# Two PSUM banks trade places in the blocks of 512 columns, and a bank's last two additions become one

## The chip, the cores and the metric

The kernel runs on one core of a Trainium2 chip. A core has a matrix engine (TensorE, PE in the profile, with its weight loads shown apart as PEld), a vector engine (VectorE, DVE), a scalar engine (ScalarE, ACT), a general engine (GpSimd, POOL) and queues that issue DMAs (SyncE, SP). Each engine runs its own list of instructions in order, and waits on semaphores for the others. TensorE writes its sums into PSUM, which holds 128 partitions of eight banks of 512 float32 values; everything else lies in SBUF. The metric is the device time of one execution in microseconds (us): the median of several runs.

## What is computed

One decoder layer on 256 tokens of width 2048, all in float32:

```
hn = rms_norm(x, norm_mix_g);  z = hn @ w_in              # 2048 x 10248
q_a, k_a, v_a, q_b, k_b, v_b, f_logit, g_a, g_b = split(z)
a   = moba_attention(q_a, k_a, v_a) @ w_proj_a            # 8 heads of 128
bfx = forgetting_attention(q_b, k_b, v_b, f_logit) @ w_proj_b
x = x + (sigmoid(g_a) * a + sigmoid(g_b) * bfx) @ w_out
hm = rms_norm(x, norm_mlp_g)
x = x + square(relu(hm @ w_up)) @ w_down                  # 2048 -> 8192 -> 2048
return rms_norm(x, norm_final_g)
```

## The kernel before

**Float32 in three products.** Every matrix product is made of pairs of rounded numbers. A value is split into a high part (a rounding copy, ScalarE, L133 for weights) and a low part (the rest, a VectorE subtraction, L148). `triple` (L324 is its matmul) then issues three matmuls of 128 rows, 128 columns and 512 moving columns: high by high, high by low, low by high. The split weights lie in rings of 12 high slots (`his`) and 10 low slots (`los`) of 512 columns each, so the splitting runs at most ten slots ahead of TensorE. Raw weights come in chunks of 1 MB through three buffers.

**Groups.** The wide products (w_in, w_up) are worked off in groups of 1024 columns. A group is a 2x2 scheme of Strassen's kind: rows are the two halves of the tokens, columns the two halves of 512. It goes through eight pairs of row blocks of the weight. A pair of kind W takes seven triples, one for each of seven PSUM banks P1 to P7, in the order P1, P2, P3, P7, P6, P4, P5 (`SEVEN_P`); of its weights the tiles T1 to T4 are sums that VectorE makes first (L160, L161, L162, `emit_sums`). A pair of kind S takes eight plain triples into P5, P3, P2 and P4. The pairs 0, 2, 4, 6 of the w_up groups are W (pairs 0, 3, 6 for w_in), the last pair is S with its triples in the order P2, P4, P2, P4, P3, P3, P5, P5 (`LAST`). Where a bank gets its last triple, `run_group` emits at once the operations that put the seven banks together to the four quarters of the row tile `c` (token half, column half): L371 on ScalarE, L372 to L381 on VectorE. P5 goes into two quarters, by L380 and L381.

**Blocks.** The narrow products (w_proj_a, w_proj_b, w_out, w_down) are worked off in blocks of 512 output columns: two banks, one for each half of the tokens, and for each 128 rows of weights a triple into the first bank and a triple into the second. The table `BANKS` says which two banks the n-th block takes. When a block is done, VectorE adds its banks to a row tile, first bank first: `proj_evac` (L707, and for the second projection L709 behind each), `out_evac` (L727), `down_part` (L759), and in the last round `final_part` (L763, L765). The eighth bank, `aux`, serves transposes and attention.

**Order.** The order on each engine is written out. `plan` is the list of groups and blocks: six w_in groups for q, k, v of both mixers; then two times two gate groups and four projection blocks (a, a, b, b); four w_out blocks; then four rounds of two w_up groups and one `run_down` of four blocks. `pump` is called after each triple and emits the splitting as soon as slots are free by the order of the program; VectorE then reaches these instructions in the order in which they were emitted. At the end of every pair (after the third and the last triple of a W pair, after the fourth and the last of an S pair) `boundary` emits small tasks that are due, one transpose task among them: after the w_out blocks these are `x1_transpose` (L736), which transposes 256 columns of the row tile that L727 has written.

**Where a block is followed by a group.** This happens five times: the gate groups follow the fourth projection block once, the first w_up group follows the fourth w_out block, and the w_up groups of rounds 2, 3 and 4 follow the fourth w_down block. The group starts with P1, P2, P3, while VectorE still has to add up the two banks of the fourth block. In all five places the fourth block has the banks `BANKS[3]`.

Of the kernel before, what the change touches and what calls it, by code (L numbers as in the profile page):

```python
# [10 lines left out]
OP = mybir.AluOpType  # L11
# [4 lines left out]
NT = 2  # L16
# [39 lines left out]
         ((0, 384, "s"), (768, 640, "v"), (384, 384, "s"), (1408, 640, "v")))  # L56
FF = 16

BANKS = (("P1", "P7"), ("P6", "P2"), ("P4", "P1"), ("P5", "P3"))


@with_exitstack
def hybrid_layer(ctx: ExitStack, tc, x, xt, gcols, w_in, w_f, b_forget, w_proj_a, w_proj_b, w_out,
                 w_up, w_down, norm_final_g, out):
    nc = tc.nc
# [98 lines left out]
    def pump(*freed):  # L164

        used.update(freed)
        while live and live[0] in used:
            used.remove(live.pop(0))
            taken[2] += 1
        go = True  # L170
        while go:
            go = False
            if acts:
                q, i = acts[0]
                names, where, _ = PIECES[chunks[q][0]][i]
                if taken[0] + len(names) - taken[2] <= HI_SLOTS and q in (sums if where else raw):
                    emit_high(q, i)
                    acts.pop(0)
                    go = True
            if dves:  # L180
                q, i = dves[0]
                names, where, _ = PIECES[chunks[q][0]][i]
                n = len(names)
                if taken[1] + n - taken[2] <= LO_SLOTS and taken[1] + n <= taken[0]:
                    emit_low(q, i)
                    dves.pop(0)
                    go = True
                else:

                    c = q + (i == len(PIECES[chunks[q][0]]) - 1)  # L190
                    if not sums and c in raw and c not in added and chunks[c][0] == "W":
                        emit_sums(c)
                        added.add(c)
                        go = True
# [10 lines left out]
    def add_block(what, src, n, k0, nk, banks):  # L205
        q = len(chunks)
        for k in range(k0, k0 + nk, 4):
            add_chunk("N", src, k, n * 512)
        plan.append(("block", what, q, nk // 4, banks))

    def add_proj(c):
        for i, (what, src) in enumerate((("pa", w_proj_a), ("pb", w_proj_b))):
            for n in (2 * c, 2 * c + 1):
                add_block((what, n), src, n, 0, NH, BANKS[2 * i + n % 2])

# [6 lines left out]
    for n in range(4):  # L222
        add_block(("o", n), w_out, n, 0, KT, BANKS[n])
    for f0 in range(0, DFF // 128, FF):
# [80 lines left out]
    def boundary():  # L305
        now[0] += 1
        due = [t for t in tasks if t[0] <= now[0]]
        tasks[:] = [t for t in tasks if t[0] > now[0]]
        for _, f, a in due:
            f(*a)  # L310
        ready = [t for t in queue if t[0] <= now[0]]
        if ready:
            t = min(ready, key=lambda t: t[0])
            queue.remove(t)
            t[1](*t[2])
# [4 lines left out]
    def triple(p, a, w, first, last):  # L320
        (xh, xl), (wh, wl) = a, w
        n = p.shape[-1]
        for j, (l, r) in enumerate(((xh, wh), (xh, wl), (xl, wh))):
            nc.tensor.matmul(p, l, r[:, :n], start=first and j == 0, stop=last and j == 2)  # L324

    def bank(n):
        return psum.tile([128, 512], FT, name=n)
# [11 lines left out]
    def run_group(q, fa, lay, plain, beside=None):  # L339

        flat = []
        for j in range(KP):
            kind = chunks[q + j][0]
            table = {"P": FOUR, "S": LAST if j == KP - 1 else EIGHT, "W": SEVEN_P}[kind]
            half = 2 if kind == "W" else 3
            flat += [(j, w, i, p, m in (half, len(table) - 1)) for m, (w, i, p) in enumerate(table)]
        last = {s[3]: m for m, s in enumerate(flat)}
        last_use = {s[:2]: m for m, s in enumerate(flat)}
        b, done, c = {}, set(), None

        def ready(*names):
            if done.issuperset(names):
                done.difference_update(names)
                return True

        for m, (j, w, i, n, end) in enumerate(flat):
            first = n not in b
            if first:
                b[n] = bank(n)
            triple(b[n], (fa[:, 0, lay.off[j] + i], fa[:, 1, lay.off[j] + i]), split[q + j, w], first, m == last[n])  # L360
            if m == last[n]:
                done.add(n)
            if last_use[j, w] == m:
                used.add((q + j, w))
            if plain:
                if end:
                    beside(j)
            else:
                if ready("P1", "P6", "P7"):
                    c = rows.tile([128, NT, 2, 512], FT, name="row")  # L370
                    nc.scalar.activation(c[:, 0, 1], b["P1"], AF.Copy)  # L371
                    nc.vector.tensor_tensor(c[:, 0, 0], b["P6"], c[:, 0, 1], OP.add)  # L372
                    nc.vector.tensor_tensor(c[:, 1, 0], c[:, 0, 0], b["P7"], OP.subtract)
                if ready("P2", "P4"):
                    nc.vector.tensor_tensor(c[:, 0, 1], c[:, 0, 1], b["P2"], OP.add)
                    nc.vector.tensor_tensor(c[:, 1, 1], c[:, 1, 0], b["P4"], OP.add)
                if ready("P3"):
                    nc.vector.tensor_tensor(c[:, 0, 0], b["P3"], c[:, 0, 0], OP.subtract)
                if ready("P5"):
                    nc.vector.tensor_tensor(c[:, 1, 0], b["P5"], c[:, 1, 0], OP.subtract)  # L380
                    nc.vector.tensor_tensor(c[:, 0, 0], c[:, 0, 0], b["P5"], OP.add)  # L381
            if m < len(flat) - 1:
                if end:
                    boundary()
                pump()
        if plain:
            c = rows.tile([128, NT, 2, 512], FT, name="row")
            for tok, h, n in ((0, 1, "P2"), (1, 1, "P4"), (1, 0, "P5"), (0, 0, "P3")):
                nc.scalar.activation(c[:, tok, h], b[n], AF.Copy)
        return c.rearrange("p t h c -> p t (h c)")  # L390
# [20 lines left out]
    def run_halves(q, act, outs, h0, h1, k0, nk, free=True):  # L411

        for h in range(h0, h1):
            for kk in range(2):
                k = k0 + 2 * (h - h0) + kk
                hi, lo = split[q + h // 2, 2 * (h % 2) + kk]
                for tok, c0, n, p in outs:
                    triple(p[:, :n], (act(k, 0, tok), act(k, 1, tok)),
                           (hi[:, c0:c0 + n], lo[:, c0:c0 + n]), k == 0, k == nk - 1)
                if free:  # L420
                    used.add((q + h // 2, 2 * (h % 2) + kk))
                if kk == 0:
                    pump()
            if h < h1 - 1:
                boundary()
                pump()
# [6 lines left out]
    def whole(ps):  # L433
        return [(tok, 0, 512, ps[tok]) for tok in range(NT)]
# [357 lines left out]
    def run_down(f0, q):  # L792
        act = pair_act(hT, f0 // 2)
        last = f0 + FF == DFF // 128
        ps = [[bank(n) for n in BANKS[i]] for i in range(2)]

        for i, (k, n) in enumerate(((0, 0), (0, 1), (8, 0), (8, 1))):
# [4 lines left out]
            pump()  # L802
        ps = [bank(n) for n in BANKS[2]]
        run_halves(q + 8, act, whole(ps), 0, 8, 0, FF)
        down_evac(2, ps, last)
        boundary()
        pump()
        ps = [bank(n) for n in BANKS[3]]
        if not last:
# [42 lines left out]
    for step, what, q, *more in plan:  # L852
        if step == "group":
            kind, n = what[:2]
            plain = more[0]
            if kind == "up" and n == 0:
                assert not [t for t in queue if t[1] is not x1_transpose]
            c = run_group(q, *((ref["x1T"], FX1) if kind == "up" else (xT, FX)), plain, forget_matmuls if plain else None)
            t0 = now[0] + 1
            if kind == "q":  # L860
# [110 lines left out]
```

## Time and profile before

| What | Value |
|---|---|
| Device time, median of 3 runs | 1377.78 us (1376.17 to 1379.2) |
| Device time of the profiled execution | 1376.19 us |
| Its span, first to last instruction | 1374.2 us |
| TensorE (PE) busy | 1349.2 us, 98% of the span, 6159 matmuls |
| VectorE busy | 1049.0 us, 76%, 1352 instructions |
| ScalarE busy | 790.9 us, 58% |
| DMA | 262.25 MB, mean 191 GB/s |
| Mean granted clock of TensorE | 0.995 of full speed |

The span is 2.0 us shorter than the time of that execution. Busy time of TensorE covers nearly the whole span, so what can go is the idle time of TensorE (25 us) and stretches in which it runs at less than full clock. A wait is charged by the profile to the instruction that released it.

### The profile page before, as it was taken

The page shows a single profiled execution, that of the slowest core. Times are in us where ns is not written, and L with a number is a line of the kernel's source. Part 1 is how long each engine was busy: PE and PEld are TensorE (multiplying, and loading weights), DVE is VectorE, ACT ScalarE, POOL GpSimd, SP SyncE. Part 2 cuts the span into 40 slices and gives each one's busy share as a digit, 9 for nine tenths or more (in the row PEclk, how much of TensorE's full clock was granted, in tenths as well). Part 3 has the DMA queues.
Part 4 walks back from the last instruction along what each step waited for, and adds up shares of the span by engine and source line. Part 5 has one row for each costly group of instructions (what it writes and reads, how often), then busy time and mean ns, then how long its engine had stood idle before and what let it go on. Part 6 is the DMA issues. An engine that isn't in the chain of part 4 may idle for free.

```text
span 1374.2 us, 16641 instructions
## 1 busy us (share of the span) xinstructions
PE 1349.2 (98%) x6159; PEld 1114.4 (81%) x6159; DVE 1049.0 (76%) x1352; ACT 790.9 (58%) x1041; POOL 13.7 (1%) x29
## 2 busy tenths in 40 slices
PE   9999999999999999999999999999999999999997
PEld 7778888888788888888788887888878888788886
DVE  5788988888967886666898567995579955799674
ACT  6766666766664465555676544665446653457532
POOL 0000000000000000000000000000000000000000
PEclk9999999999999999999999999999999999999999
DMA  8556554544565656564557554566545665555651
GB/s 309 183 188 212 184 170 166 184 153 158 184 211 168 209 206 215 201 228 153 170 198 240 184 189 158 187 216 206 186 151 184 217 212 186 180 185 202 232 199 72
DMA packets 93824, 262.25 MB, mean 191 GB/s; under 512 B 4656, under 2 KB 5040, under 8 KB 93104
## 3 DMA queue, kind: packets, MB, share of 16 engines
q1 hardware_dynamic: 92752, 257.97, 55.2%
q10 hardware_dynamic: 992, 3.24, 0.6%
q8 instruction: 48, 0.79, 0.2%
q14 instruction: 32, 0.26, 0.1%
HBM read 259.09 MB, written 2.10 MB: 190 GB/s over the span
## 4 chain that ended last, share of the span: by engine, by line
PE 91%; DVE 3%; ACT 3%; issue 1%; DMA 1%; POOL 0%; SPq 0%; POOLq 0%; ACTq 0%; DVEq 0%
PE P L324 87%; PE aux L667 2%; DMA raw<-in_w_in_dram 1%; ACT his L133 1%; DVE los L148 1%; DVE sum L160 1%; PE aux L641 1%; PE aux L593 0%; PE aux L627 0%; DVE row L759 0%; DVE sum L161 0%; ACT pr L448 0%; ACT row L469 0%; PE aux L642 0%; PE aux L736 0%
## 5 line engine op out<-in xcount | busy, mean ns | idle before, releaser
L324 PE MATMUL P<-his,big 128*128 128x512 f32 x2186 | 706.6, 397 | 12.1 <-DVE row L759 7.0
L133 ACT ACTIVATE his<-raw 128x1024 fp32r<-128x1024 f32 (+1 forms) x525 | 480.6, 932 | 380.0 <-PE P L324 357.8
L148 DVE TENSOR_TENSOR los<-raw,his 128x1024 fp32r<-128x1024 f32 (+1 forms) x579 | 550.0, 983 | 150.1 <-PE P L324 109.4
L324 PEld LDWEIGHTS P<-his,big 128*128 128x128 f32 x2186 | 412.8, 189 | 101.0 <-DVE row L759 8.3
L324 PE MATMUL P<-his,pr 128*128 128x512 f32 (+1 forms) x1568 | 483.5, 387 | 0.0
L324 PE MATMUL P<-los,big 128*128 128x512 f32 x1093 | 427.9, 392 | 0.3 <-DVE los L485 0.3
L324 PEld LDWEIGHTS P<-his,pr 128*128 128x128 f32 x1568 | 292.3, 188 | 58.2
L324 PE MATMUL P<-los,pr 128*128 128x512 f32 (+1 forms) x784 | 302.0, 385 | 0.0
L324 PEld LDWEIGHTS P<-los,big 128*128 128x128 f32 x1093 | 206.7, 189 | 41.4 <-DVE los L485 0.6
L324 PEld LDWEIGHTS P<-los,pr 128*128 128x128 f32 x784 | 147.4, 188 | 28.5
L148 DVE TENSOR_TENSOR los<-sum,his 128x1024 fp32r<-128x1024 f32 (+1 forms) x139 | 143.9, 1060 | 30.2 <-PE P L324 29.0
L133 ACT ACTIVATE his<-sum 128x1024 fp32r<-128x1024 f32 (+1 forms) x129 | 124.8, 981 | 48.2 <-PE P L324 27.9
L160 DVE TENSOR_TENSOR sum<-raw 128x1024 f32<-128x1024 f32 x59 | 72.0, 1221 | 0.4 <-DMA raw<-in_w_up_dram 0.3
L755 DVE TENSOR_TENSOR pr<-tmp,pr 128x512 fp32r<-128x512 f32 x32 | 22.1, 689 | 29.7 <-ACT pr L754 29.7
L161 DVE TENSOR_TENSOR sum<-sum,raw 128x512 f32<-128x512 f32 x59 | 41.7, 706 | 2.0
L162 DVE TENSOR_TENSOR sum<-sum,raw 128x512 f32<-128x512 f32 x59 | 40.8, 692 | 2.0
L667 PEld LDWEIGHTS aux<-ident,row 128*128 128x128 f32 x224 | 28.0, 141 | 9.1 <-ACT cum L566 2.1
L667 PE MATMUL aux<-ident,row 128*128 128x128 f32 x224 | 33.6, 272 | 1.6 <-ACT cum L566 1.6
L752 ACT ACTIVATE tmp<-aux 128x512 f32<-128x512 f32 x32 | 19.2, 599 | 26.3 <-PE aux L667 26.1
L396 DVE TENSOR_TENSOR big<-pr,big 128x512 fp32r<-128x512 f32 (+1 forms) x16 | 10.5, 658 | 23.9 <-ACT big L395 23.9
L759 DVE SCALAR_TENSOR_TENSOR row<-P,inv,row 128x512 f32<-128x512 f32 x24 | 17.1, 749 | 11.0 <-PE P L324 11.0
L407 ACT ACTIVATE big<-pr 128x256 fp32r<-128x256 f32 (+1 forms) x16 | 8.2, 510 | 23.7 <-DVE pr L406 13.9
(133 smaller groups left out, 511.4 us busy)
## 6 DMA issues: line engine op xcount, KB each, us to landing
raw<-in_w_in_dram SPq DMA_DIRECT2D x79, 1024.0 KB, 5.2
raw<-in_w_up_dram SPq DMA_DIRECT2D x64, 1024.0 KB, 5.1
raw<-in_w_down_dram SPq DMA_DIRECT2D x64, 1024.0 KB, 5.2
raw<-in_w_out_dram SPq DMA_DIRECT2D x16, 1024.0 KB, 5.2
raw<-in_w_proj_a_dram SPq DMA_DIRECT2D x8, 1024.0 KB, 5.2
raw<-in_w_proj_b_dram SPq DMA_DIRECT2D x8, 1024.0 KB, 5.2
row<-in_xt_dram SPq DMA_DIRECT2D x8, 256.0 KB, 8.5
row<-in_x_dram SPq DMA_DIRECT2D x2, 1024.0 KB, 7.9
```

The lines of the kernel that those rows point to most:

```text
L133: nc.scalar.activation(his[:, s:s + m], src[:, j:j + m], AF.Copy)
L148: nc.vector.tensor_tensor(los[:, s + jj:s + jj + mm], src[:, j + jj:j + jj + mm], his[:, h:h + mm].bitcast(FT), OP.subtract)
L160: nc.vector.tensor_tensor(t[:, 0:2], r[:, 1:3], r[:, 0:1].to_broadcast([128, 2, 512]), OP.add)
L161: nc.vector.tensor_tensor(t[:, 2], t[:, 0], r[:, 2], OP.add)
L162: nc.vector.tensor_tensor(t[:, 3], t[:, 2], r[:, 3], OP.add)
L324: nc.tensor.matmul(p, l, r[:, :n], start=first and j == 0, stop=last and j == 2)
L396: nc.vector.tensor_tensor(fa[:, 1, o + i:o + 4], f[:, i:4], fa[:, 0, o + i:o + 4].bitcast(FT), OP.subtract)
L641: nc.tensor.matmul(p[:, i * S:(i + 1) * S], v[:, 0, sl], pt[:, :S], start=True, stop=False)
L667: nc.tensor.transpose(p[:, c, s * 128:(s + 1) * 128], src[:, tok, (i + c) * 128:(i + c + 1) * 128], ident)
L752: nc.scalar.activation(t, p, AF.Square)
L755: nc.vector.tensor_tensor(h[:, :, 1], t, h[:, :, 0].bitcast(FT), OP.subtract)
L759: nc.vector.scalar_tensor_tensor(t, p, inv2[:, tok:tok + 1], t, op0=OP.mult, op1=OP.add)
```

## The change

The table `BANKS` gives the third block P3 and P1 instead of P4 and P1, and the fourth block P4 and P5 instead of P5 and P3. In `run_group` the sign of the quarter `c[:, 1, 0]` is turned round, so that the last bank P5 is added to both quarters with the same sign; L380 and L381 become one VectorE operation of 2 x 512 elements, in which P5 is the second operand, repeated along the new axis.

```diff
-BANKS = (("P1", "P7"), ("P6", "P2"), ("P4", "P1"), ("P5", "P3"))
+BANKS = (("P1", "P7"), ("P6", "P2"), ("P3", "P1"), ("P4", "P5"))
...
-                    nc.vector.tensor_tensor(c[:, 1, 0], c[:, 0, 0], b["P7"], OP.subtract)
+                    nc.vector.tensor_tensor(c[:, 1, 0], b["P7"], c[:, 0, 0], OP.subtract)
...
-                    nc.vector.tensor_tensor(c[:, 1, 1], c[:, 1, 0], b["P4"], OP.add)
+                    nc.vector.tensor_tensor(c[:, 1, 1], b["P4"], c[:, 1, 0], OP.subtract)
...
                 if ready("P5"):
-                    nc.vector.tensor_tensor(c[:, 1, 0], b["P5"], c[:, 1, 0], OP.subtract)
-                    nc.vector.tensor_tensor(c[:, 0, 0], c[:, 0, 0], b["P5"], OP.add)
+                    p5 = b["P5"].rearrange("p (o c) -> p o c", o=1).to_broadcast([128, NT, 512])
+                    nc.vector.tensor_tensor(c[:, :, 0], c[:, :, 0], p5, OP.add)
```

**TensorE, from the last w_down block of a round to the w_up group behind it.** `P5_5964` is bank P5 as the block uses it, `P1_6096` bank P1 as the group uses it; in brackets stands the engine whose semaphore the instruction waits for. Of each triple that only goes on, the rows are left out. Before:

```order
L324 MATMUL P5_5964<-his_78,pr_5672 128x512
L324 MATMUL P3_5965<-his_78,pr_5672 128x512
...
L324 MATMUL P1_6096<-his_78,big_4411 128x512 [waits Activation_49]
...
L324 MATMUL P2_6103<-his_78,big_4411 128x512 [waits Activation_49]
...
L324 MATMUL P3_6107<-his_78,big_4411 128x512 [waits DVE_49]
...
L324 MATMUL P7_6113<-his_78,big_4411 128x512 [waits Activation_49]
...
L324 MATMUL P6_6122<-his_78,big_4411 128x512
...
L324 MATMUL P4_6126<-his_78,big_4411 128x512 [waits Activation_49]
...
L324 MATMUL P5_6130<-his_78,big_4411 128x512
```

In the changed kernel the same stretch of TensorE's list reads:

```order
L324 MATMUL P4_5953<-his_78,pr_5661 128x512
L324 MATMUL P5_5954<-his_78,pr_5661 128x512
...
L324 MATMUL P1_6085<-his_78,big_4402 128x512 [waits Activation_49]
...
L324 MATMUL P2_6092<-his_78,big_4402 128x512 [waits Activation_49]
...
L324 MATMUL P3_6096<-his_78,big_4402 128x512
L324 MATMUL P3_6096<-los_79,big_4402 128x512
...
L324 MATMUL P7_6102<-his_78,big_4402 128x512 [waits Activation_49]
L324 MATMUL P7_6102<-los_79,big_4402 128x512 [waits DVE_49]
...
L324 MATMUL P6_6111<-his_78,big_4402 128x512
...
L324 MATMUL P4_6115<-his_78,big_4402 128x512 [waits DVE_49,Activation_49]
...
L324 MATMUL P5_6119<-his_78,big_4402 128x512 [waits DVE_49]
```

The matmuls stand in the same order; the wait for VectorE that stood at the third triple (P3) now stands at the sixth and seventh (P4, P5), and the fourth has a wait of its own for its low part.

**TensorE, from the last w_out block to the first w_up group.** Here a transpose (`aux`, L736) of the row that the block's evacuation writes comes behind the third triple. Before:

```order
L324 MATMUL P3_4918<-his_78,big_4411 128x512 [waits DVE_49]
L324 MATMUL P3_4918<-los_79,big_4411 128x512
L324 MATMUL P3_4918<-his_78,big_4411 128x512
L736 MATMUL aux_4925<-ident_119,row_4322 128x128 [waits PE_49,Activation_49]
L736 MATMUL aux_4925<-ident_119,row_4320 128x128
```

And in the changed kernel:

```order
L324 MATMUL P3_4909<-his_78,big_4402 128x512
L324 MATMUL P3_4909<-los_79,big_4402 128x512
L324 MATMUL P3_4909<-his_78,big_4402 128x512
L736 MATMUL aux_4916<-ident_119,row_4313 128x128 [waits DVE_49,Activation_49]
L736 MATMUL aux_4916<-ident_119,row_4311 128x128
```

The wait for VectorE has moved by one triple, from P3 to the transpose.

**VectorE, at the end of a group.** The piece of the difference at the first group with seven banks; the numbers behind P name the banks' buffers, `P_638` is P5:

```order
-L376 TENSOR_TENSOR row<-row,P_634 128x512
+L376 TENSOR_TENSOR row<-P_634,row 128x512
 L378 TENSOR_TENSOR row<-P_610,row 128x512
 L148 TENSOR_TENSOR los<-sum,his 128x1024
-L380 TENSOR_TENSOR row<-P_638,row 128x512
-L381 TENSOR_TENSOR row<-row,P_638 128x512
```

One instruction of 2 x 512 (L381) stands where two of 512 stood, in each of the 17 groups with seven banks. On VectorE nothing else changes its place, and on ScalarE and SyncE nothing at all.

## Rows read from the trace of the kernel before

**Rows 1.** The page, part 1, and one group of part 5.

```profile
PE 1349.2 (98%) x6159; PEld 1114.4 (81%) x6159; DVE 1049.0 (76%) x1352; ACT 790.9 (58%) x1041; POOL 13.7 (1%) x29
...
L759 DVE SCALAR_TENSOR_TENSOR row<-P,inv,row 128x512 f32<-128x512 f32 x24 | 17.1, 749 | 11.0 <-PE P L324 11.0
```

**Rows 2.** Waits of TensorE: engine line waited for: total us, times, longest.

```profile
PE P L324 <- DVE row L759: 7.0, 3, 2.3
PE P L324 <- DVE row L727: 2.2, 1, 2.2
...
PE P L324 <- DVE row L707: 0.4, 1, 0.4
```

**Rows 3.** Timeline, start of round 2: start, us, engine, line, shapes, [idle before].

```profile
835.37 0.39 PE L324 MATMUL P<-los,pr 128*128 128x512 f32 x1
...
836.05 0.39 PE L324 MATMUL P<-los,pr 128*128 128x512 f32 x1
836.31 1.22 DVE L160 TENSOR_TENSOR sum<-raw 128x1024 f32<-128x1024 f32 x1
...
837.63 0.39 PE L324 MATMUL P<-his,big 128*128 128x512 f32 x1
838.90 1.40 DVE L759 SCALAR_TENSOR_TENSOR row<-P,inv,row 128x512 f32<-128x512 f32 x2
840.22 1.82 DVE L148 TENSOR_TENSOR los<-raw,his 128x1024 fp32r<-128x1024 f32 x2
840.36 0.50 PE L324 MATMUL P<-his,big 128*128 128x512 f32 x1 [2.34 <-DVE row L759]
```

**Rows 4.** Windows: length, busy (x instructions) of each engine, PEclk, DMA share, GB/s.

```profile
840.36:845.03 4.67, 4.67 (x13) 3.67 (x14) 3.50 (x4) 2.10 (x3) 0.00 (x0) 0.63 0.54 174
1017.04:1022.41 5.37, 5.37 (x16) 4.25 (x17) 3.09 (x4) 2.00 (x2) 0.00 (x0) 0.68 0.59 197
1193.73:1198.19 4.46, 4.46 (x19) 3.68 (x20) 4.04 (x5) 2.67 (x3) 0.00 (x0) 1.00 0.46 150
```

**Rows 5.** Timeline, last w_out block and first w_up group.

```profile
661.77 0.39 PE L324 MATMUL P<-his,big 128*128 128x512 f32 x1
663.03 1.28 DVE L727 TENSOR_TENSOR row<-row,P 128x512 f32<-128x512 f32 x2
664.37 0.50 PE L324 MATMUL P<-his,big 128*128 128x512 f32 x1 [2.21 <-DVE row L727]
...
665.17 0.60 PE L736 MATMUL aux<-ident,row 128*128 128x128 f32 x4
```

**Rows 6.** Timeline, last projection block and the gate group behind it.

```profile
440.95 0.39 PE L324 MATMUL P<-his,big 128*128 128x512 f32 x1
440.95 0.68 DVE L707 TENSOR_TENSOR row<-row,P 128x512 f32<-128x512 f32 x1
441.69 0.50 PE L324 MATMUL P<-his,big 128*128 128x512 f32 x1 [0.35 <-DVE row L707]
```

**Rows 7.** Timeline, VectorE at the end of a w_up group.

```profile
882.14 0.69 DVE L380 TENSOR_TENSOR row<-P,row 128x512 f32<-128x512 f32 x1
882.74 0.68 DVE L381 TENSOR_TENSOR row<-row,P 128x512 f32<-128x512 f32 x1
883.33 1.22 DVE L148 TENSOR_TENSOR los<-raw,his 128x1024 fp32r<-128x1024 f32 x1
```

**Rows 8.** Windows: a gate group; w_up groups of rounds 1, 2, 2, 4.

```profile
441.00:486.00 45.00, 44.65 (x197) 36.71 (x196) 38.56 (x47) 24.59 (x28) 0.00 (x0) 1.00 0.54 187
664.40:704.00 39.60, 39.60 (x179) 32.80 (x180) 36.36 (x48) 25.22 (x35) 0.00 (x0) 1.00 0.55 188
840.40:882.00 41.60, 41.60 (x176) 34.23 (x177) 35.41 (x40) 22.11 (x25) 0.00 (x0) 0.96 0.58 199
882.00:926.00 44.00, 44.00 (x203) 36.46 (x202) 42.08 (x52) 31.75 (x40) 0.00 (x0) 1.00 0.56 195
1193.70:1233.00 39.30, 39.27 (x173) 32.52 (x174) 34.29 (x39) 21.48 (x24) 0.00 (x0) 1.00 0.58 204
```

## The prediction

> **What bounds the kernel now.** I began with the page's busy times: TensorE works 1349.2 us of a span of 1374.2, VectorE 1049.0 [rows 1]. So the matmuls set the time, and what an edit can give is TensorE's 25 us of idle time and what its clock loses. The second view was the list of TensorE's waits. Three lines name exactly the evacuations behind which a group follows a block: L759 three times, 7.0 us, L727 once, 2.2, L707 once, 0.4; together 9.6 of the 25 [rows 2]. The third view, the timeline around them, shows why. In round 2 the block's last low-part matmul starts at 836.05, the group's second triple issues its last matmul at 837.63, and the third, which writes P3, starts at 840.36 after 2.34 us of idle time. Meanwhile VectorE makes the weight sums L160 to L162 from 836.31 on, and only then, at 838.90, the two L759, P5 first and P3 second [rows 3]. TensorE starts 0.06 us after the second has ended (838.90 + 1.40 = 840.30). The wait is thus for the second of two evacuations, which stand in VectorE's queue behind three instructions nobody is in a hurry for.
>
> The fourth view, windows behind these waits, shows a second cost. After the waits of rounds 2 and 3 the granted clock of the next 4.67 and 5.37 us is 0.63 and 0.68 on the mean, that is, most of it at 1.2 GHz; after an equal wait in round 4 it is 1.00 [rows 4].
>
> **The banks.** A triple takes 0.68 us (835.37 to 836.05), a matmul 0.23 [rows 3]. Without the wait, P3's triple would start at 837.63 + 0.23 = 837.86; it starts at 840.36, so 2.50 us are lost, 0.16 more than the idle time that is shown. The three waits are equal (7.0 us for 3, the longest 2.3 [rows 2]), so with the same 0.16 each of rounds 2 to 4 loses 2.50, 7.5 in all. Then the clock: 13 matmuls take 4.67 us where 13 x 0.228 = 2.96 would do, loss 1.71; 16 take 5.37 instead of 3.65, loss 1.72; in round 4, 19 take 4.46 instead of 4.33, loss 0.13 for the restart alone [rows 4]. The three rounds: 7.50 + 3.56 = 11.06 us.
>
> What is late next? In the changed order P3 was emptied a block earlier, and the wait moves to P4, the sixth triple, and P5, the seventh. P4's triple is due 3 triples behind 837.86, at 839.91; its L759 starts at 838.90 and takes 0.75 [rows 1], so P4 is free at 839.65 + 0.06 = 839.71. P5's triple is due at 840.60, and P5 is free where P3 was, at 840.36. Both are in time, by 0.20 and 0.24 us. That is little, but both ends hang on the same matmuls: VectorE's sums start when TensorE frees slots of the ring, before anything has changed. If the margin were missed, the cost is the few tenths by which it is missed.
>
> Behind it VectorE's splitting is next. The L148 at 840.22 makes low parts of pair 1's second half [rows 3]; TensorE needs them in the fifth triple of pair 1, nine triples behind P3's: 837.86 + 9 x 0.68 = 844.0. They are there at 841.4. The whole pair 0 has been split before the group begins, for the ring holds ten slots, and the last three w_down slots and the seven of pair 0 fill it. So nothing stands in the way in the first pairs. Over the whole group VectorE idles 41.60 - 35.41 = 6.2 us in round 2 and 39.30 - 34.29 = 5.0 us in round 4 [rows 8]; TensorE will be 4.2 and 2.6 us faster there, which leaves VectorE 2.0 and 2.4 us. It can still catch up and fill its ring.
>
> At the first w_up group the gain is nearly all lost again: behind P3's triple stands the transpose L736 of the very row that the two L727 write. P3's triple will run at 662.0, but the transposes start at 664.37 (663.03 + 1.28 + 0.06) instead of 665.17 [rows 5]: 0.80 us saved of a wait of 2.21, and a new wait of about 1.7 on L736. At the gate group the third triple was due at 440.95 + 0.23 = 441.18 and came at 441.69 [rows 6], 0.51 lost, with the restart 0.11 more: 0.6 us.
>
> Everywhere else the two banks are taken long after they were freed: blocks follow blocks there, and P1 keeps its place as the second bank of the third block.
>
> **The merged operation.** L380 and L381 run from 882.14 to 883.42, 1.28 us for both, and the next one starts at 883.33, 1.19 behind the first [rows 7]. The merged form does not occur before. The nearest row is a two-tensor operation on 1024 elements from SBUF, 1.22 us [rows 7]; two single ones with no overlap, 0.69 + 0.68 = 1.37, is the other end. I take 1.22: about 0.06 us per group less, 1.0 us of VectorE over 17 groups, at most 1.5 more. On TensorE's path it is worth nothing: P5's next triple is the seventh of the following group, over 4 us behind, and no wait in the list is for L380 or L381. Without that cover 1.37 would cost 17 x 0.09 = 1.5 us, and 1.22 give 1.0. The swapped operands of L373 and L376 keep the shape; I put them at zero.
>
> **Sum.** 11.06 + 0.80 + 0.62 = 12.5 us. The profiled execution took 1376.19, 2.0 us more than its span, and nothing in those 2.0 changes; that gives 1363.7. It is the lower end of the three runs, and the median lies 1.6 us above it. That is just one more lost clock (1.7), so I expect most of that distance to go with the waits, and predict 1364.3.
>
> **Rivals.**
> 1. VectorE becomes the bound in the groups. For it: it works 42.08 of 44.00 us in the second group of round 2 [rows 8], and in the first groups only 2.0 to 2.4 us of slack will be left. Against: not one wait of TensorE for low parts in these groups. If the time gained on the wait is paid back later in the group, 7.5 us return: 1371.2.
> 2. The same mechanism on the other side: TensorE runs ahead, meets an empty ring in both w_up groups of rounds 2 to 4, and every such wait costs the clock as well. The place is L148 before a W pair's sums; the price is 7.5 us given back and in six groups 1.7 of clock, 17.7 in all, so 1381.4. It decides as soon as VectorE is over 2.4 us late within a group.
> 3. The clock falls without the long waits. Rows 4 show a fall behind two of three equal waits, so the wait is not the whole cause; the three waits' falls may come elsewhere, above all behind the new waits of a few tenths and at L736. Price as in rows 4, 1.71 + 1.72: 1367.1.
> 4. The wait only moves. Were VectorE 2.3 us later at P4 and P5, as some other queue entry ahead of L759 could make it, nothing but the 0.8 and 0.6 would be won: 1374.8 from the profiled execution, 1376.4 from the median.
>
> By the Trainium skill, "TensorE: Matmul & The Clock Gate", section "What's actually happening", the half clock is the default and activity lifts it; by that rule a shorter wait can only help, as in rows 4, and the 3.4 us stay won. Its section "A second HAM failure mode: psum-queue depth-cycling" speaks against: there small idle times between groups of matmuls that cycle through PSUM banks were enough to make the clock swing. By that rule rival 3 holds. The trace bears the first out more: the groups behind the two shorter waits, of 0.35 and 2.21 us, ran at a granted clock of 1.00 throughout [rows 5, 6, 8].
>
> **Chances.** Forecast 0.77, rival 1 0.07, rival 3 0.09, rival 4 0.04, rival 2 0.03. Cases above 1369 hold about 0.13, so the range goes from 1361.0 (the sum with all of the merged operation's gain and a little of what runs differ) to 1369.0. A change of 0.2%, 2.8 us, is about what a measurement can tell from none here. Faster: forecast, rivals 1 and 3, 0.93; same: rival 4, 0.04; slower: rival 2, 0.03.
>
> **What would show it.** Right: the list of TensorE's waits without L759 and L707 lines, or with tenths of a us; L727's line replaced by one for L736 of about 1.7 us; granted clock 1.00 in the 10 us behind the starts of rounds 2 to 4; L381 at 17 x about 1.22 us; TensorE idle 17 us instead of 25. Wrong: waits for L148 inside w_up groups (rivals 1, 2), clock falls without a wait ahead (rival 3), waits of 2 us at P4 (rival 4), L381 over 1.4 us.

## The result and the profile after

The changed kernel takes 1363.22 us (median of 4 runs, 1363.06 to 1363.85) where the kernel before, beside it on the chip, takes 1378.25: a ratio of 0.9894, 95% interval 0.9877 to 0.9911, 15.0 us. The profiled execution took 1363.29 us against 1376.19 before: 12.9 us. The forecast was 1364.3, from a sum of 12.5. Two executions behind the table of experiments below took two and nearly four times as long as the others (2758 and 5081 us) and are left out of its medians and ratios.

Busy times on the page of the changed kernel (share of the span, instructions), to [rows 1]:

```profile
PE 1345.5 (99%) x6159; PEld 1113.2 (82%) x6159; DVE 1046.0 (77%) x1335; ACT 790.3 (58%) x1041; POOL 13.7 (1%) x29
```

The span is 1361.5 us, 12.7 shorter. TensorE idles 16.0 us instead of 25.0, and it is busy 3.7 us less for the same 6159 matmuls; 3.4 of that is the clock it lost behind two of the waits ([rows 4]: 1.71 and 1.72). Of the 9.0 us of idle time 8.0 are the waits that the change is about; the rest lies in small waits in the first 75 us (such as L389, 0.9 us before), which come and go between profiles of one kernel. The list of TensorE's waits (engine, line, waited for: us, times, longest), to [rows 2]:

```profile
PE aux L736 <- DVE row L727: 1.6, 1, 1.6
```

The lines for L759, L707 and for a bank behind L727 are gone; this one, of the transposes, is new. Round 2's start in the timeline (start, us, engine, line), to [rows 3]:

```profile
834.81 1.22 DVE L160 TENSOR_TENSOR sum<-raw 128x1024 f32<-128x1024 f32 x1
...
836.58 0.39 PE L324 MATMUL P<-los,big 128*128 128x512 f32 x1
...
837.39 1.41 DVE L759 SCALAR_TENSOR_TENSOR row<-P,inv,row 128x512 f32<-128x512 f32 x2
...
838.63 0.40 PE L324 MATMUL P<-los,big 128*128 128x512 f32 x1
...
839.32 0.39 PE L324 MATMUL P<-los,big 128*128 128x512 f32 x1
```

Everything up to L759 stands 1.50 us earlier, at the same distances. TensorE goes through P3 (836.58 is its low part), P7, P6, P4 (838.63) and P5 (839.32) in steps of 0.68 us: the evacuations at 837.39, for which it waited before, now end (838.80) while it works. Windows as long as those of [rows 4] in the same stretch, the first from 0.2 us ahead of P3's triple, the others from 1.2 and 1.8 us behind its start (length, busy and instructions of PE, PEld, DVE, ACT, POOL, then PEclk, DMA share, GB/s):

```profile
836.16:840.83 4.67, 4.67 (x22) 3.83 (x21) 4.64 (x7) 2.91 (x4) 0.00 (x0) 1.00 0.00 0
1010.00:1015.37 5.37, 5.37 (x25) 4.40 (x24) 5.37 (x7) 3.79 (x5) 0.00 (x0) 1.00 0.36 93
1183.00:1187.50 4.50, 4.50 (x21) 3.66 (x21) 4.50 (x7) 3.27 (x4) 0.00 (x0) 1.00 0.34 81
```

22, 25 and 21 matmuls where 13, 16 and 19 stood, and the clock at 1.00 in all three; over the 10 us of 834 to 844, 1008 to 1018 and 1181 to 1191, each of which begins ahead of P3's triple, it is 1.00 too. At the first w_up group ([rows 5]):

```profile
661.64 0.39 PE L324 MATMUL P<-his,big 128*128 128x512 f32 x1
...
662.23 1.28 DVE L727 TENSOR_TENSOR row<-row,P 128x512 f32<-128x512 f32 x2
...
663.65 0.63 PE L736 MATMUL aux<-ident,row 128*128 128x128 f32 x4 [1.62 <-DVE row L727]
664.04 0.48 PE L324 MATMUL P<-his,big 128*128 128x512 f32 x1
```

P3's triple no longer waits, but the transposes do, 1.62 us, as the price of moving the wait one triple on.

To see where the time was won, one compares the same instruction in both traces. These are the first L707 of the fourth projection block and the L160 at the start of rounds 1, 3 and 4, first before, then after:

```profile
439.63 0.68 DVE L707 TENSOR_TENSOR row<-row,P 128x512 f32<-128x512 f32 x1
...
660.44 1.22 DVE L160 TENSOR_TENSOR sum<-raw 128x1024 f32<-128x1024 f32 x1
...
1013.00 1.22 DVE L160 TENSOR_TENSOR sum<-raw 128x1024 f32<-128x1024 f32 x1
...
1189.68 1.22 DVE L160 TENSOR_TENSOR sum<-raw 128x1024 f32<-128x1024 f32 x1
```

```profile
439.48 0.68 DVE L707 TENSOR_TENSOR row<-row,P 128x512 f32<-128x512 f32 x1
...
659.64 1.22 DVE L160 TENSOR_TENSOR sum<-raw 128x1024 f32<-128x1024 f32 x1
...
1007.25 1.22 DVE L160 TENSOR_TENSOR sum<-raw 128x1024 f32<-128x1024 f32 x1
...
1179.70 1.22 DVE L160 TENSOR_TENSOR sum<-raw 128x1024 f32<-128x1024 f32 x1
```

The distances grow from 0.15 to 0.80, 1.50 (836.31 in [rows 3], 834.81 above), 5.75 and 9.98, and the span ends 12.7 earlier. So the gate group gave 0.65 us, the first w_up group 0.70, round 2's start 4.25, round 3's 4.23, round 4's 2.7; 0.15 came from the start.

The merged operation, of the groups of instructions (xcount | busy, mean ns | idle before):

```profile
L381 DVE TENSOR_TENSOR row<-row,P 128x1024 f32<-128x1024 f32 x17 | 20.7, 1215 | 0.0
```

VectorE's windows from the first splitting in the group on, to [rows 8] (both groups of round 2, the first of round 4):

```profile
838.90:876.25 37.35, 37.35 (x166) 30.93 (x165) 34.77 (x40) 20.45 (x23) 0.00 (x0) 1.00 0.64 222
876.25:920.25 44.00, 44.00 (x203) 36.45 (x202) 42.02 (x51) 31.74 (x40) 0.00 (x0) 1.00 0.55 195
1183.70:1220.30 36.60, 36.60 (x163) 30.28 (x163) 33.96 (x39) 19.83 (x23) 0.00 (x0) 1.00 0.65 217
```

VectorE idles 2.6, 2.0 and 2.6 us in these groups, and TensorE does not wait for it.

### The profile page after: what moved, and what is told of

The parts are those of the page before. It is cut to its first block, busy times and chain, and to the rows that moved or that the text cites. A ratio compares the mean times of both kernels' runs of the same rounds, so it can differ in the third digit from the quotient of the medians.

```text
span 1361.5 us, 16621 instructions
## 1 busy us (share of the span) xinstructions
PE 1345.5 (99%) x6159; PEld 1113.2 (82%) x6159; DVE 1046.0 (77%) x1335; ACT 790.3 (58%) x1041; POOL 13.7 (1%) x29
## 4 chain that ended last, share of the span: by engine, by line
PE 93%; ACT 3%; DVE 2%; DMA 1%; issue 1%; POOL 0%; SPq 0%; POOLq 0%; ACTq 0%; DVEq 0%
PE P L324 88%; PE aux L667 2%; DMA raw<-in_w_in_dram 1%; ACT his L133 1%; DVE los L148 1%; PE aux L641 1%; PE aux L593 0%; PE aux L627 0%; ACT pr L448 0%; ACT row L469 0%; PE aux L736 0%; PE aux L642 0%; DVE sum L160 0%; PE aux L592 0%; ACT big L407 0%
## 5 line engine op out<-in xcount | busy, mean ns | idle before, releaser
L133 ACT ACTIVATE his<-raw 128x1024 fp32r<-128x1024 f32 (+1 forms) x525 | 480.8, 932 | 371.4 <-PE P L324 351.9
L148 DVE TENSOR_TENSOR los<-raw,his 128x1024 fp32r<-128x1024 f32 (+1 forms) x579 | 549.4, 982 | 144.9 <-PE P L324 101.8
L148 DVE TENSOR_TENSOR los<-sum,his 128x1024 fp32r<-128x1024 f32 (+1 forms) x139 | 143.2, 1058 | 25.1 <-PE P L324 24.8
L133 ACT ACTIVATE his<-sum 128x1024 fp32r<-128x1024 f32 (+1 forms) x129 | 124.5, 981 | 45.2 <-PE P L324 26.4
L160 DVE TENSOR_TENSOR sum<-raw 128x1024 f32<-128x1024 f32 x59 | 71.9, 1219 | 0.8 <-DMA raw<-in_w_in_dram 0.7
L759 DVE SCALAR_TENSOR_TENSOR row<-P,inv,row 128x512 f32<-128x512 f32 x24 | 17.1, 749 | 11.0 <-PE P L324 11.0
```

The source lines that it names most:

```text
L133: nc.scalar.activation(his[:, s:s + m], src[:, j:j + m], AF.Copy)
L148: nc.vector.tensor_tensor(los[:, s + jj:s + jj + mm], src[:, j + jj:j + jj + mm], his[:, h:h + mm].bitcast(FT), OP.subtract)
L160: nc.vector.tensor_tensor(t[:, 0:2], r[:, 1:3], r[:, 0:1].to_broadcast([128, 2, 512]), OP.add)
L759: nc.vector.scalar_tensor_tensor(t, p, inv2[:, tok:tok + 1], t, op0=OP.mult, op1=OP.add)
```

## The experiments

| Kernel | Median us | Kernel before beside it | Ratio, 95% interval |
|---|---|---|---|
| Banks alone | 1363.67 | 1377.35 | 0.9902 (0.9887 to 0.9918) |
| Merged operation alone | 1377.07 | 1377.35 | 0.9998 (0.9989 to 1.0006) |
| Old banks, sums behind the evacuations | 1362.55 | 1377.35 | 0.9896 (0.9880 to 0.9911) |
| New banks, sums behind the evacuations | 1361.84 | 1377.35 | 0.9890 (0.9876 to 0.9903) |
| Changed kernel, P5 ahead of P4 | 1365.00 | 1377.32 | 0.9913 (0.9900 to 0.9927) |
| Changed kernel again | 1363.31 | 1377.32 | 0.9901 (0.9886 to 0.9916) |
| New banks, sums behind, again | 1361.72 | 1377.32 | 0.9890 (0.9876 to 0.9903) |
| Kernel before, longer wait | 1383.11 | 1377.32 | 1.0043 (1.0031 to 1.0056) |
| Kernel before, P3 ahead of P5 | 1369.90 | 1376.59 | 0.9950 (0.9936 to 0.9963) |

**Which half of the change pays.** The banks alone:

```diff
-BANKS = (("P1", "P7"), ("P6", "P2"), ("P4", "P1"), ("P5", "P3"))
+BANKS = (("P1", "P7"), ("P6", "P2"), ("P3", "P1"), ("P4", "P5"))
```

> The new order of the banks alone; L380 and L381 stay two operations with the old signs. Theory (the gain is the waits on P3 and the clock lost behind them; the merged operation is hidden): 1363.2 to 1364.2 us, no wait of TensorE on L759 or L707, one of about 1.6 us of L736 on L727. Rival (VectorE is so nearly the bound in the groups that the 17 shorter operations pay on the path): slower than the changed kernel by 1 us or more, 1364.3 to 1367, with waits for L148.

1363.67 us: the forecast of the theory, and the list of waits is the expected one, 1.6 us of L736 on L727 and none on L759 or L707. With the two operations kept apart (groups of instructions again)

```profile
L380 DVE TENSOR_TENSOR row<-P,row 128x512 f32<-128x512 f32 x17 | 11.6, 684 | 0.0
L381 DVE TENSOR_TENSOR row<-row,P 128x512 f32<-128x512 f32 x17 | 11.5, 678 | 0.0
```

TensorE waits for neither. The merged operation alone, with the old table:

> The merged operation alone, the banks in the old order. Theory: no change from before, 1376 to 1379 us, L759's waits of TensorE 7.0 us as before. Rival (the merged operation pays on the path): 1 to 2 us faster than before. In both, runs of this kernel and of before differ among each other by steps of about 1.7 us, a lower mean clock with the longer time.

1377.07, no change that can be told, with the old waits, L759's the largest of them:

```profile
PE P L324 <- DVE row L759: 7.0, 3, 2.3
```

The steps of 1.7 us that the expectation speaks of do not show: the eleven executions lie between 1375.2 and 1378.25, and their mean clock (0.995 or 0.996) does not order them. So the gain is the banks', as far as these runs can tell. The 17 pairs' durations add up to 23.1 us against 20.7 of the merged operation, but the two of a pair overlapped ([rows 7]: 1.28 us for both, where the merged one takes 1.215), so VectorE is relieved of 1.2 us (busy 1049.0 on the page before, 1047.8 with the merged operation alone), and nobody waits for that.

**What the wait is for.** Here the banks stay in the old order, and only the sums for a later pair are kept back until the evacuations have been issued:

```diff
-    def pump(*freed):
+    def pump(*freed, hold=False):
...
-                    if not sums and c in raw and c not in added and chunks[c][0] == "W":
+                    if not hold and not sums and c in raw and c not in added and chunks[c][0] == "W":
...
-    def run_halves(q, act, outs, h0, h1, k0, nk, free=True):
+    def run_halves(q, act, outs, h0, h1, k0, nk, free=True, hold=False):
...
-                    pump()
+                    pump(hold=hold and h == h1 - 1)
...
-            run_halves(q + 12, act, whole(ps), 0, 8, 0, FF)
+            run_halves(q + 12, act, whole(ps), 0, 8, 0, FF, hold=True)
...
-                run_halves(q, pair_act(merged), whole(ps), 0, 2 * nch, 0, 4 * nch)
+                run_halves(q, pair_act(merged), whole(ps), 0, 2 * nch, 0, 4 * nch, hold=n == 3)
```

> The kernel before, with its banks and its two operations; only the sums L160 to L162 are issued behind the two evacuations of the last block instead of ahead of them, in the four places where a w_up group follows a block (the gate group stays as it was). Theory (the wait is for evacuations that stand behind sums that are not needed yet): P3 would be free at about 837.77 in round 2, where its triple is due at 837.86, so the three waits and the wait at the first w_up group all go: 7.5 + 3.6 + 2.5 us, 1361.5 to 1364, as fast as the changed kernel or 1 us faster. Rival (the bank's order is what matters, or the sums are needed at once): little gain, 1372 to 1378, or new waits for L133 or L148 on sums in pair 2 of the groups.

1362.55: as the theory has it. Of the five waits only L707's 0.4 us at the gate group is left, which this edit does not touch. Round 2's start in its timeline:

```profile
833.61 1.41 DVE L759 SCALAR_TENSOR_TENSOR row<-P,inv,row 128x512 f32<-128x512 f32 x2
...
834.92 1.22 DVE L160 TENSOR_TENSOR sum<-raw 128x1024 f32<-128x1024 f32 x1
834.93 0.64 PE L324 MATMUL P<-his,big 128*128 128x512 f32 x2
...
835.40 0.40 PE L324 MATMUL P<-los,big 128*128 128x512 f32 x1
```

The two L759 run ahead of L160 and end at 835.02. P3's triple begins with the second of the two matmuls from 834.93 on, at 835.16, and its low part follows at 835.40: the pace of 0.23 us is kept, nothing waits. The bank's place in the table is thus not what matters by itself; it is whether VectorE has emptied the bank when its turn comes, and that can be had by the order of the banks or by the order of VectorE's queue.

The same with the new banks, to win the wait of L736 as well:

> The changed kernel with the sums issued behind the evacuations in the same four places. Theory: only the wait of L736 on L727, 1.6 us, is left to win: 1361.4 to 1362.0, about 1.6 us faster than the changed kernel. Rival (TensorE then runs into a VectorE that is too late with its sums, since its slack in the first groups is 2.0 to 2.4 us): no gain, with waits for L148 or for L133's high parts of sums.

1361.84. Beside the changed kernel on one chip:

> The changed kernel with the sums issued behind the evacuations, once more, to set it against the changed kernel on the same chip. Theory: 1.6 us faster, the wait of L736 on L727. Rival (VectorE's slack is used up and part of it is paid back in the groups): 0 to 0.8 us.

> The changed kernel once more, beside the others on the same chip: 1363 to 1364 us, no wait on L759.

1361.72 (1361.43 to 1362.22) against 1363.31 (1363.04 to 1363.72): 1.59 us faster than the changed kernel, in the place that was expected. At the first w_up group:

```profile
659.70 1.28 DVE L727 TENSOR_TENSOR row<-row,P 128x512 f32<-128x512 f32 x2
...
661.70 0.39 PE L324 MATMUL P<-his,big 128*128 128x512 f32 x1
661.93 0.60 PE L736 MATMUL aux<-ident,row 128*128 128x128 f32 x4
```

The two L727 run at 659.70, L160 behind them from 660.90 on, and L736 follows P3's triple at once, 661.93. This is the fastest version here: the banks and the queue's order together take out all five waits. The rival shows a little in one of its two profiles: in that of the second run TensorE waits 0.16 us for L378 at 703.33, at the end of the first w_up group, and from its first matmul of round 1 to that of round 2 it takes 174.14 us (659.89 to 834.03) where the first run's profile has 173.58 (660.02 to 833.60).

**How tight the margin is.** The changed kernel with the fourth block's banks swapped:

```diff
-BANKS = (("P1", "P7"), ("P6", "P2"), ("P3", "P1"), ("P4", "P5"))
+BANKS = (("P1", "P7"), ("P6", "P2"), ("P3", "P1"), ("P5", "P4"))
```

> The changed kernel with the two banks of the fourth block in the other order, P5 first, P4 second; so P4 comes free with the second evacuation and is wanted by the sixth triple. Theory (the margin was 0.20 us at P4 and 0.24 us at P5, so 0.44 us are missing now): three waits of TensorE on L759, about 0.3 us each as the profile shows them, with the restart 0.5 us each on the path, 1.5 us more than the changed kernel: 1364.5 to 1365.2 if that reads 1363.2. The clock stays up behind such short waits. Rival (short idle times make the clock fall as long ones do): 1.7 us more for each fall, 1366 to 1370.

1365.00, 1.69 us over the changed kernel beside it. Round 3's start:

```profile
1011.10 0.39 PE L324 MATMUL P<-his,big 128*128 128x512 f32 x1
1011.88 0.47 PE L324 MATMUL P<-his,big 128*128 128x512 f32 x1 [0.39 <-DVE row L759]
```

0.39 us idle, and 0.78 from one matmul to the next where 0.23 is the pace: 0.55 lost at each of three places, 1.65 in all. (In round 2 the profile puts the same 0.39 us down to a copy on ScalarE, L133, in rounds 3 and 4 to L759.) The margin of 0.2 us was real, and a step of 0.65 us in VectorE's order uses it up. The clock did not fall: it is 1.00 in the 5 us behind each of the three.

**What the clock does behind waits of other lengths.** First shorter: the old table with P3 ahead of P5.

```diff
-BANKS = (("P1", "P7"), ("P6", "P2"), ("P4", "P1"), ("P5", "P3"))
+BANKS = (("P1", "P7"), ("P6", "P2"), ("P4", "P1"), ("P3", "P5"))
```

> The kernel before with the fourth block's two banks in the other order, P3 first, P5 second; nothing else is changed. P3 comes free with the first evacuation, 0.65 us sooner, and P5 is wanted four triples later. Theory: the three waits shrink from 2.34 to about 1.7 us, 1.95 us in all; the waits of the gate group and of the first w_up group give 0.6 us each; at least 3.2 us less than before, 1374 where before reads 1377.4, and as much less again as falls of the clock (1.7 us each) become rarer behind a wait of 1.7 us: down to 1371. Rival (the clock falls behind a wait of any length alike): 1374 to 1375 with as many falls as before.

1369.90, 6.7 us less than before. Its waits on L759:

```profile
PE P L324 <- DVE row L759: 5.0, 3, 1.7
```

and the windows behind them:

```profile
838.81:843.50 4.69, 4.69 (x20) 3.87 (x21) 4.68 (x6) 2.99 (x4) 0.00 (x0) 1.00 0.38 114
...
1187.67:1192.40 4.73, 4.73 (x21) 3.91 (x22) 4.68 (x6) 2.95 (x3) 0.00 (x0) 1.00 0.38 106
```

The waits are 2.0 us shorter in all (7.0 in [rows 2]), and the gate group and the first w_up group give 1.2, as expected: from the first L707 of the fourth projection block to the L160 of round 2 it is 395.4 us (439.99 to 835.43), before 396.7 (439.63 to 836.31). The rest, some 3.5 us, is about what two falls of the clock take, 1.7 each: 1.00 behind all three waits (the first and the last are shown), 20 to 21 matmuls in 4.7 us. Then longer, with one more multiplication of 512 columns ahead of each of the two evacuations:

```diff
-                down_part(n, ps[tok], tok)
+                n == 3 and nc.vector.tensor_tensor(tmp(), x1[tok][:, :512], x1[tok][:, :512], OP.mult); down_part(n, ps[tok], tok)
```

> The kernel before with one more VectorE multiplication of 512 columns (its result is not used) ahead of each of the two evacuations of the fourth w_down block in rounds 1 to 3, so that P3 comes free later by about 1.3 us. Theory: the three waits grow from 2.34 to about 3.6 us, 3.9 us in all, and the clock falls behind all three instead of about two of three: 1381 to 1384 where before reads 1377 to 1378. Rival A (the fall has nothing to do with the wait's length): two of three falls as before, 1381. Rival B (the ring fills while TensorE waits and the time is made good): under 1379.

1383.11, 5.8 us more than before. The waits on L759 are now

```profile
PE P L324 <- DVE row L759: 10.6, 3, 3.5
```

and behind every one of them the clock is down (rounds 2 and 4 shown, 0.70 in round 3):

```profile
842.67:847.40 4.73, 4.73 (x15) 3.81 (x16) 3.60 (x4) 2.10 (x3) 0.00 (x0) 0.68 0.55 178
...
1197.93:1202.70 4.77, 4.77 (x11) 3.80 (x12) 3.67 (x4) 2.11 (x2) 0.00 (x0) 0.50 0.54 173
```

Three waits longer by 1.2 us are 3.6, and a third fall 1.7: 5.3 of the 5.8. The sum is rough, since the falls were not all alike: behind round 4's wait the clock stayed down longer (22 matmuls in the 8 us from 1197.93 on, clock 0.61, where behind the other two waits 29 fit, clock 0.81 and 0.82), and in this profile it was down behind the unchanged wait of 2.21 us on L727 as well (0.66 in 664.00 to 669.00).

**Why the median moved by more than the profiled execution.** Three more profiles of the kernel before, with nothing changed:

> The kernel before, unchanged, for one more profile. Theory (its runs differ by the number of the three waits behind which the clock falls, 1.7 us each): a profiled time near 1376 goes with two falls, one near 1377.7 with three. Rival (the longer runs lose their time elsewhere): two falls in a run near 1377.7.

> As the run before it: near 1376 us two falls of the clock behind the three waits, near 1377.7 us three; by the rival the number of falls and the time do not go together.

> As the two runs before it: near 1376 us two falls of the clock behind the three waits, near 1377.7 us three; by the rival the number of falls and the time do not go together.

They took 1376.65, 1377.59 and 1377.71 us. Windows of 5 us behind the four long waits (the w_out block's, then rounds 2 to 4), first of the run of 1376.65, then of the run of 1377.71:

```profile
665.07:670.07 5.00, 5.00 (x24) 4.16 (x25) 2.97 (x8) 3.16 (x10) 0.00 (x0) 1.00 0.59 188
841.06:846.06 5.00, 5.00 (x15) 4.00 (x16) 3.50 (x4) 2.10 (x3) 0.00 (x0) 0.66 0.57 184
1017.74:1022.74 5.00, 5.00 (x15) 3.98 (x16) 2.90 (x3) 2.00 (x2) 0.00 (x0) 0.66 0.57 181
1194.46:1199.46 5.00, 5.00 (x22) 4.11 (x23) 4.13 (x6) 3.07 (x3) 0.00 (x0) 1.00 0.56 179
```

```profile
664.55:669.55 5.00, 5.00 (x17) 4.02 (x18) 2.97 (x8) 3.09 (x9) 0.00 (x0) 0.66 0.56 183
842.18:847.18 5.00, 5.00 (x15) 3.97 (x16) 3.50 (x4) 2.10 (x3) 0.00 (x0) 0.66 0.56 187
1018.85:1023.85 5.00, 5.00 (x22) 4.11 (x23) 4.21 (x5) 3.19 (x4) 0.00 (x0) 1.00 0.57 177
1193.95:1198.95 5.00, 5.00 (x15) 3.94 (x16) 3.60 (x4) 2.11 (x2) 0.00 (x0) 0.66 0.58 174
```

Two falls in the one, three in the other; the run of 1377.59 has three as well. But the third is not where I had expected it, and on this the expectation failed and its rival was right. In all five profiles with three waits of 2.34 us the clock fell behind just two of the three (rounds 2 and 3, or 2 and 4); what comes and goes is the fall behind the wait of 2.21 us on L727 at the first w_up group. It is there in the two longer runs, and missing in the three of 1376.1 to 1376.7 (the first profile, that of 1376.65, and that of the merged operation alone). With it, round 1 takes 1.6 us longer: 177.50 us from the first matmul of its first group to that of round 2 in the run of 1377.71, 175.87 in that of 1376.65. The changed kernel has no wait of either length, so it would win such a fall too where one comes, 1.7 of the 2.1 us between the 12.9 of the profiled executions and the 15.0 of the medians. For the medians this is inferred: the executions that make them up have no profile. Beside the changed kernel's second run, on another chip, the kernel before took 1377.32, and the gain was 14.0 us.

## Why the prediction was right

- **The three waits, 4.21 + 4.22 + 2.63 = 11.06 us:** measured 4.25, 4.23 and 2.7. Both terms held, the idle time with its 0.16 and the clock counted in matmuls. The experiment with the old banks and later sums showed the cause: the wait went away without a bank being moved.
- **What is late next:** P4 and P5 came in time, as worked out, by 0.20 and 0.23 us in the trace after; with the two reversed, P4 is freed 0.65 us later than worked out, and of the 0.45 that then are missing 0.39 showed as idle time, and 0.55 was lost.
- **The first w_up group, 0.80 us, and the new wait of 1.7 on L736:** measured 0.70 and 1.62. But the term was mis-sized for the median: the wait it replaced, 2.21 us, costs the clock in some executions, 1.7 us more, and the one profile at hand showed one without. The sentence that the group behind this wait ran at 1.00 throughout was thus true of that execution alone: behind the same wait the clock fell in two of the five profiles with the old waits, and in that with the longer ones. I had put the 1.6 us between profile and median down to "one more lost clock" and let most of it go with the waits. The size came out right; but no row showed where that fall would be, and the place that I had in mind in the experiments, a third fall behind the three L759, was wrong. That the median came within 1.1 us of the forecast is in this part luck.
- **The gate group, 0.62 us:** 0.65.
- **The merged operation, 1.22 us and nothing on the path:** 1.215, VectorE's busy time fell by 1.2 us where 1.0 was forecast, and alone it gave 0.3 us of 1377, inside its interval.
- **VectorE's slack, 2.0 and 2.4 us:** 2.6 and 2.6. Rivals 1 and 2 lived on that slack; no wait for L148 appeared. In one profile of the fastest version there is one of 0.2 us, but it stands at 15.29, far ahead of the changed places, and a profile of the kernel before has one of 0.3 at 15.94; it says nothing of the slack. The wait of 0.16 us for L378 in that profile does.
- **Rival 3, falls without long waits:** none in the changed kernel, where the clock is 1.00 from 14 us to 1358 us, and none behind the waits of 0.39 and 1.68 us. Its page's rule, the Trainium skill, "TensorE: Matmul & The Clock Gate", section "A second HAM failure mode: psum-queue depth-cycling", is thus not borne out for the short idle times of this kernel; the rule of its section "What's actually happening", that the half clock is the default state and activity lifts it, agrees with what the runs show: the matmuls of the first microseconds come 0.43 us apart and later 0.23, and the clock is down behind the idle times of 3.54 us. Rival 4 fell with the first list of waits.
- **The chances:** the cases above 1369 add up to 0.14 (0.07, 0.04 and 0.03), not 0.13.

The sum from the profile (1363.7) was nearer to the median of 1363.2 than the 1364.3 that I gave: once the waits are gone, the runs differ by 0.8 us (1363.06 to 1363.85) where those before differed by 3.0.

## What to carry to other kernels

When TensorE waits for a bank, look at what stands ahead of the evacuation in the evacuating engine's queue, and at which triple wants the bank first: a bank that the next stage wants late, or an evacuation ahead of work that nobody needs yet, each removes the wait whole. Then follow the next reader of the same data, here a transpose one triple on, for it inherits the wait. And price a wait of TensorE with the clock behind it, counted over several executions: here 2.3 us of idle time cost 2.7 or 4.2 us, and a wait cut to 1.7 us cost 2.0, with no clock lost behind it (round 2 took 174.42 us from its first w_up matmul to that of round 3, in the changed kernel 172.44).

## What the runs showed of the hardware that I had not expected

Behind waits of one length the clock was steadily split: of three waits of 2.34 us exactly two were followed by 1.2 GHz in five profiles of five, behind 1.68 us none of three, behind 3.54 us three of three. Behind the 2.21 us at the first w_up group it was three profiles of six, and behind the 1.61 or 1.62 us that stand there with P3 first or with the new banks none of five. What picks the one that goes free is left open here.

The row of the granted clock can miss a stretch at half the clock. At the start of the changed kernel's trace the matmuls come 0.43 us apart instead of 0.23, with no idle time between them,

```profile
10.77 1.05 PE L324 MATMUL P<-his,big 128*128 128x512 f32 x2
11.63 0.63 PE L324 MATMUL P<-los,big 128*128 128x512 f32 x1
```

while the window over them says 1.00. In the kernel before the same matmuls come at this pace too, and there the row says 0.57 (first the window after, then before):

```profile
8.00:12.00 4.00, 4.00 (x10) 3.08 (x10) 1.73 (x4) 2.33 (x6) 0.00 (x0) 1.00 1.04 413
8.00:12.00 4.00, 4.00 (x13) 3.13 (x12) 1.76 (x4) 2.26 (x5) 0.00 (x0) 0.57 1.02 410
```

The count of matmuls (10 in 4 us, where 17 or 18 fit) tells it; the clock is therefore best read together with that count.
